# Output projection of a retention layer: ordinary products in phase one and block products in phase two, with the sums of phase two made under phase one

## The chip, the cores and the metric

The kernel runs on one core of a Trainium2 chip. The metric is the device time of one execution in microseconds (us), as the median of several runs. A lower time is better. The engines are named as in the profile: PE is TensorE (matmul), PEld its weight load, DVE is VectorE, ACT is ScalarE, POOL is GpSimd, and SP is SyncE, which here only issues DMAs.

## The reference, cut to what matters

The model has two layers in f32, one of retention and one of sliding-window attention (SWA), for a prompt of 1024 tokens and eight single decode tokens. Only the retention layer and the first thing that SWA does are touched by the change.

```python
def retention_layer(x, S0, g_norm, w_in, g_out, w_out):
    h = rmsnorm(x, g_norm)
    q, k, v, gate = split(h @ w_in)          # 4 heads, DK = 256, DV = 512
    o, S = retention_scan(q, k, v, S0)       # per chunk of 128 tokens and head:
    #   inner = (q k^T) * decay mask;  o = inner v + (q S) * decay;  S = g S + (k*decay)^T v
    o = rmsnorm(o, g_out) * silu(gate)       # width 4 * 512 = 2048
    return x + o @ w_out, S                  # w_out: 2048 x 1024
```

`o @ w_out` has 2048 inputs per token (four heads of 512) and 1024 outputs. The next layer starts with `rmsnorm(x) @ w_in_swa`.

## The kernel before, in words

**Numbers in two parts.** Every f32 operand of a product is split into a high part (type fp32r, made by a copy, mostly on ACT) and a low part (value minus high part, on POOL or DVE), and a product is three matmuls: high by high, high by low, low by high.

**Stages.** (1) The input projection of retention, to about 537 us of the span. (2) The retention itself, 32 steps: a step is one chunk of 128 tokens of one head; first heads 0 and 1 alternate over eight chunks (steps 0 to 15), then heads 2 and 3 (steps 16 to 31). (3) The output projection, eight sets. (4) SWA, from 886.6 us.

**A retention step.** On PE: the state's update (`S`, L998 to L1000), the output (`po`, L1002 to L1011), then three groups of products into PSUM tiles named `tr`: the transposes of the normalised output `on` of the step before (L104), the product of k and q of a coming chunk (L776) and its transposes. PSUM has two `tr` buffers. On the other engines, in the order that `others` (L1065) writes them: DVE multiplies the transposed output of step i-2 by the gate (`og`, L1062), makes the low part of the state (`Sl`, L1030), the mean square (`bss`, L1041; its power -0.5 is POOL's L119), the score tile `sT` (L793), the normalised output `on` (L1049) and the low part of k (`kl`, L788). POOL makes the low parts of v, of the scores and of q (L813, L803, L825). ACT makes the high parts. The order on every engine is the order of the program; nothing is reordered.

**The output projection.** The eight sets are two phases of four: phase one multiplies the gated output of heads 0 and 1 by its half of `w_out`, phase two that of heads 2 and 3. Set a of a phase makes the output columns 256 a to 256 a + 255, for all 1024 tokens in two halves t = 0, 1, with decode columns beside them. In a set the weight piece is a 2 x 2 block of quarters A11, A12, A21, A22, and the tokens' side is a 2 x 2 block B11, B12, B21, B22 (head by even or odd chunks).

- An *ordinary* set (`p_plain`, L1282) has eight slots of 24 matmuls, 192 in all; its weights are the four quarters.
- A *block* set (`p_prod`, L1263) uses the scheme with seven products instead of eight: 14 slots of 12 matmuls, 168 in all. It needs sums of weight quarters (S1 to S4, `p_sum`, on POOL) and sums of the tokens' side (T1 to T4), and its results are combined by more additions (`p_evac` and `p_pre`).

The operands of the tokens' side lie in seven cells for each t (in the tiles SA and SB), called B11, T2, T1, B21, T3, B22, T4. Before the change sets 4 and 5 (the first two of phase two) are ordinary, and the six others are block sets. So T1 to T4 of heads 0 and 1 have to exist when phase one begins: `x_items` (L1080) spreads that work over steps 6 to 31 in four portions. A portion reads the gated chunks that DMAs have put into the cells, makes four sums on DVE in the tile G0 (the rows `G<-G,SA` and the like of L1549), seven high parts on ACT and seven low parts on POOL (L1549). For phase two the gated chunks go to DRAM (`osc`) and come back; `split` and `t_sums` turn them into cells in sets 3 to 6.

**The plan.** `p_plan` (L1400) gives each slot a time by its count of matmuls, and each piece of work on ACT, DVE, POOL and SP a due time or a slot (`when`, `later`); the pieces are then written into the program between the slots in that order. Of set 0, `p_early` (L1502) prepares the weight pieces A11, S1, S2 and A12 under the last retention steps. `p_xr` (L1205) loads the residual input x of a set, four DMAs of 128 KB each for one t, and `p_xt` (L1210) transposes it on DVE into the tiles that the slot results are added to (names evc, evw, evx, evp in the profile, and rx, rp); before the change both halves go through one tile, `xr`. Sets of phase one leave partial results in DRAM, which sets of phase two load.

**Other work in set 7.** `kv_raw` and `kv_conv` (L1388, L1394) load and split the weights of SWA's keys and values (rows `kv<-ra,kv`, L1398). `a_load` and `a_split` (L1360, L1363) reload the normalised result of the layer and split it for SWA (DVE rows of L1369).

## Time and profile before

| what | value |
|---|---|
| time, median of 3 runs | 1325.73 us (1324.01 to 1327.58) |
| the profiled execution's own time | 1328.74 us |
| its span in the profile | 1326.9 us |
| mean granted PE clock | 0.986 |
| PE busy | 1275.2 us, 96% of the span |
| DVE, ACT, POOL busy | 790.1, 682.7, 797.9 us |
| retention, first state product to the first product of set 0 | 537.20 to 696.40 us |
| the eight sets of the output projection | 696.40 to 886.60 us |

Times in the trace count from the start of the span. A row of the timeline has a start, a duration, engine, line, operation and tiles, and in brackets the idle time of its engine just before it with what ended it (`<-`). A row of the windows has the stretch, its length, and for each engine busy time and count of instructions, then the granted PE clock as a share of full speed, the share of the DMA engines' time and GB/s.

### The profile page before, as it was taken

How to read it: one execution, taken by the hardware profiler on the slowest of the kernel's cores; microseconds unless marked ns; L12 is line 12 of the kernel's file. 1: busy time of each engine (PE TensorE's matmuls, PEld its weight loads, DVE VectorE, ACT ScalarE, POOL GpSimd, SP SyncE). 2: the span in 40 equal slices, each digit the busy share in tenths (PEclk: the TensorE clock that was granted, in tenths of full speed). 3: DMA queues.
4: the chain of work that ended last, by engine and by line, in shares of the span. 5: the costliest groups of instructions: out<-in, count | busy, mean ns of one | idle time of the engine just before them, and what ended most of it. 6: DMA issues, size and time to landing. Idle time of an engine off the chain costs nothing.

```text
span 1326.9 us, 26895 instructions
## 1 busy us (share of the span) xinstructions
PE 1275.2 (96%) x9767; PEld 1217.6 (92%) x9767; DVE 790.1 (60%) x1511; ACT 682.7 (51%) x1686; POOL 797.9 (60%) x935
## 2 busy tenths in 40 slices
PE   6999999999999999899898999989998999999998
PEld 6999999999999999777778989979998999998998
DVE  6944555666566763477674568584565666766321
ACT  5532445454455563578772244456576666666121
POOL 6654534555468998679895676556476766554000
PEclk9999999999999999899998999989998999999999
DMA  6314777667676863478756586543032111227232
GB/s 225 101 60 143 220 218 227 200 214 227 202 215 188 236 201 110 140 241 253 237 183 174 145 264 198 172 156 109 17 96 80 57 55 46 81 95 260 73 95 77
DMA packets 230322, 208.79 MB, mean 157 GB/s; under 512 B 32889, under 2 KB 206197, under 8 KB 230173
## 3 DMA queue, kind: packets, MB, share of 16 engines
q1 hardware_dynamic: 198192, 172.71, 43.2%
q10 hardware_dynamic: 31996, 34.36, 7.9%
q8 instruction: 77, 1.26, 0.4%
q14 instruction: 57, 0.46, 0.1%
HBM read 134.36 MB, written 69.50 MB: 154 GB/s over the span
## 4 chain that ended last, share of the span: by engine, by line
PE 78%; POOL 6%; DVE 5%; issue 4%; DMA 4%; ACT 2%; SPq 1%; POOLq 0%; ACTq 0%; DVEq 0%
PE b L334 8%; PE b L335 7%; PE b L336 7%; PE pj L1634 6%; PE pj L1635 5%; PE pj L1636 5%; PE b L327 4%; PE b L328 4%; PE b L329 4%; PE S L1293 3%; PE tr L104 3%; PE o L1997 2%; PE b L543 2%; PE S L336 1%; PE S L334 1%
## 5 line engine op out<-in xcount | busy, mean ns | idle before, releaser
L334 PE MATMUL b<-xh,woh 128*128 128x258 f32 x784 | 223.2, 285 | 0.0
L336 PE MATMUL b<-xh,wol 128*128 128x258 f32 x784 | 221.7, 283 | 0.0
L335 PE MATMUL b<-xl,woh 128*128 128x258 f32 x784 | 221.6, 283 | 0.0
L1634 PE MATMUL pj<-SA,wh 128*128 128x384 f32 (+1 forms) x512 | 175.0, 342 | 1.7 <-ACT SA L2017 1.3
L1635 PE MATMUL pj<-SA,wh 128*128 128x384 f32 (+1 forms) x512 | 164.8, 322 | 0.2 <-DVE SA L2018 0.2
L1636 PE MATMUL pj<-SA,wl 128*128 128x384 f32 (+1 forms) x512 | 164.7, 322 | 0.0
L334 PEld LDWEIGHTS b<-xh,woh 128*128 128x128 f32 x784 | 148.0, 189 | 4.1 <-issue 3.7
L335 PEld LDWEIGHTS b<-xl,woh 128*128 128x128 f32 x784 | 148.7, 190 | 0.0
L336 PEld LDWEIGHTS b<-xh,wol 128*128 128x128 f32 x784 | 148.0, 189 | 0.0
L225 POOL TENSOR_TENSOR wol<-raw,woh 128x512 fp32r<-128x512 f32 x52 | 68.0, 1316 | 119.8 <-ACT woh L220 108.6
L327 PE MATMUL b<-woh,xh 128*128 128x256 f32 x448 | 126.6, 283 | 0.0
L328 PE MATMUL b<-wol,xh 128*128 128x256 f32 x448 | 126.0, 281 | 0.0
L329 PE MATMUL b<-woh,xl 128*128 128x256 f32 x448 | 125.6, 280 | 0.0
L1634 PEld LDWEIGHTS pj<-SA,wh 128*128 128x128 f32 x512 | 97.1, 190 | 5.4 <-issue 2.6
L1635 PEld LDWEIGHTS pj<-SA,wh 128*128 128x128 f32 x512 | 97.3, 190 | 0.4 <-DVE SA L2018 0.4
L1636 PEld LDWEIGHTS pj<-SA,wl 128*128 128x128 f32 x512 | 96.9, 189 | 0.0
L1975 POOL TENSOR_TENSOR s<-s,sm 128x512 f32<-128x512 f32 x64 | 66.6, 1040 | 48.3 <-DVE sm L1974 44.1
L327 PEld LDWEIGHTS b<-woh,xh 128*128 128x128 f32 x448 | 84.3, 188 | 5.0 <-issue 2.9
L329 PEld LDWEIGHTS b<-woh,xl 128*128 128x128 f32 x448 | 84.3, 188 | 0.0
L328 PEld LDWEIGHTS b<-wol,xh 128*128 128x128 f32 x448 | 84.3, 188 | 0.0
L1967 ACT ACTIVATE s<-s,mx 128x257 f32<-128x257 f32 x128 | 64.2, 505 | 34.6 <-DVE mx L1965 33.8
L220 ACT ACTIVATE woh<-s 128x512 fp32r<-128x512 f32 x88 | 54.1, 624 | 53.3 <-POOL s L210 22.8
(543 smaller groups left out, 3823.6 us busy)
## 6 DMA issues: line engine op xcount, KB each, us to landing
raw<-in_w_in_ret_dram ACTq DMA_DIRECT2D x44, 512.0 KB
st<-in_state_ret_dram SPq DMA_DIRECT2D x64, 256.0 KB
out_dram<-st SPq DMA_DIRECT2D x64, 256.0 KB
vb<-vscr SPq DMA_DIRECT2D x64, 128.0 KB
evp<-qks SPq DMA_DIRECT2D x32, 256.0 KB
evx<-vsc SPq DMA_DIRECT2D x32, 256.0 KB
wr<-in_w_in_swa_dram SPq DMA_DIRECT2D x32, 256.0 KB
evc<-gsc SPq DMA_DIRECT2D x16, 256.0 KB
```

What stands on the lines that cost most here:

```text
L225: eng.tensor_tensor(lo, src_of(s, name, sub), hi.bitcast(F32), SUB)
L327: mm(dst, xh, wh, start=a and i == 0, stop=False, skip_group_check=True)
L328: mm(dst, xh, wl, start=False, stop=False, skip_group_check=True)
L329: mm(dst, xl, wh, start=False, stop=z, skip_group_check=True)
L334: mm(dst, wh, xh, start=a, stop=False, **sg)
L335: mm(dst, wh, xl, start=False, stop=False, **sg)
L336: mm(dst, wl, xh, start=False, stop=z, **sg)
L1634: mm(ps, hi[:, k, fs], xh[:, k, t0:t1], start=first and k == ks[0], stop=False)
L1635: mm(ps, hi[:, k, fs], xl[:, k, t0:t1], start=False, stop=False)
L1636: mm(ps, lo[:, k, fs], xh[:, k, t0:t1], start=False, stop=last and k == ks[-1])
L1967: nc.scalar.activation(st[:, j, :], st[:, j, :], AF.Exp, bias=mx[:, j:j + 1], accum_out=sm[:, j:j + 1])
L1975: nc.gpsimd.tensor_tensor(st[:, :, 0:256], st[:, :, 0:256], sm.unsqueeze(2).broadcast_to([128, 2, 256]), ALU.mult)
```

## The change

1. **The two phases change kind.** Sets 0 to 3 (phase one) are ordinary and sets 4 to 7 (phase two) are block sets.
2. **No sums under the retention.** `x_items` is gone. Each gated chunk of heads 0 and 1 stays in SBUF (`OG`) and is split right away into one cell by one ACT copy (`b_oh`) and one POOL subtraction (`b_ol`), two steps later than its products, 16 of each. The DMAs that put these chunks into the cells are gone.
3. **The sums of phase two are made under phase one.** The chunks of heads 2 and 3 are loaded from DRAM in sets 0 and 1 (2 MB into the cells T1 and T2, 2 MB into the two G tiles), and `t_sums`, now in six parts, makes T1, T2, T4 and a scratch copy of T3 in sets 1 and 2. B11 and B21 are split in set 3, T3 and B22 in set 4.
4. **Set 0 is prepared further.** `p_early` at steps 20 to 30 loads the raw weights, makes all four quarters (high on ACT, low on POOL) and loads x for t = 0 into a tile of its own (`acc`); x for t = 1 is loaded when the projection's tiles open. What belongs to the end of the retention comes after slot 0 instead of slot 1.
5. **Retention's buffers** are laid out one by one (`lay`), in a given order, which changes the addresses that they share with tiles of stage 1; the last two loads of v and gate of the start (`b_v(3)`, `b_g(3)`) are issued at step 0 instead of at the end of stage 1.
6. **SWA's key and value weights** are loaded and split in set 5 instead of set 7. Their raw tile is `xr`.
7. Smaller ones: x loads of sets 1 to 3 are issued 18 and 17 us ahead instead of 9 and 3 (`p_plan`'s time); `p_pre` is split into three; two of SWA's first small products are issued ahead of their loop.

The diff, cut to its core:

```diff
...
-    for fn, n in ((b_v, 2), (b_q, 3), (b_g, 2), (b_v, 3), (b_g, 3)):
+    for fn, n in ((b_v, 2), (b_q, 3), (b_g, 2)):
...
+    lay("Sh1", "Sl1", "sT0", "sTh0", "sTl0", "on0", "qh0", "ql0", "kh0", "kl0", "sT1", "ss0", "ss1", "vl0",
+        "on1", "vh1", "vl1", "kh1", "kl1", "pad", "Sh0", "Sl0", "vh0", "qh1", "ql1", "sTh1", "sTl1")
...
+        o_ = ogt[h % 2] if h >= 2 else OG[:, (2 * c + h) % 4]
         dve.tensor_tensor(o_, d.pop(("pt", c)).rearrange("p (i t) -> p i t", i=4), d["g", c], MUL)
-        nc.sync.dma_start(out=(osc[h - 2, par, t] if h >= 2 else raw_of(((B11, T1), (B21, B22))[h][par], t))[:, :, cs], in_=o_)
+        if h >= 2:
+            nc.sync.dma_start(out=osc[h - 2, c % 2, c // 4][:, :, 128 * (c // 2 % 2):128 * (c // 2 % 2) + 128], in_=o_)
+        d["og", c] = o_
+
+    def b_oh(h, c):
+        if h < 2:
+            act(at_cell(h, c)[0], heads[h]["og", c], AF.Copy)
+
+    def b_ol(h, c):
+        if h < 2:
+            hi, lo = at_cell(h, c)
+            pool.tensor_tensor(lo, heads[h]["og", c], hi.bitcast(F32), SUB)
...
-                      [(b_on, i - 1)] + conv[3:]):
+                      [(b_on, i - 1)] + conv[3:] + [(b_oh, i - 2), (b_ol, i - 2)]):
...
-        dec_sums(dT, 0)
...
-    def x_items(q, i0):
...
-        ta, tb, tc_ = [G0[:, 512 * j:512 * j + 512].rearrange("p (k f) -> p k f", k=4) for j in (q % 3, (q + 1) % 3, (q + 2) % 3)]
-        src = {B11: r[B11], B21: r[B21], B22: r[B22], T1: ta, T2: tb, T3: tc_, T4: ta}
...
-        for i, o_, x, y in ((0, ta, r[T1], r[B11]), (1, tb, r[B22], ta), (2, tc_, tb, r[B11]), (4, ta, r[B21], tb)):
-            put(i, dve.tensor_tensor, o_, x, y, SUB)
-        for i, x in enumerate((B22, T1, T2, B11, T3, B21, T4)):
-            put(i, act, XH[t][x][:, :, cs], src[x], AF.Copy)
-            put(i + 2, pool.tensor_tensor, XL[t][x][:, :, cs], src[x], XH[t][x].bitcast(F32)[:, :, cs], SUB)
...
-        s.n, s.P, s.a, s.kind, s.fw, s.plain = n, n // 4, n % 4, "p", 128, n in (4, 5)
+        s.n, s.P, s.a, s.kind, s.fw, s.plain = n, n // 4, n % 4, "p", 128, n < 4
...
+    def xr_tile(t):
+        return acc[:, 0:1024].rearrange("p (n f) -> p n f", n=16) if t == 0 else pq["xr"]
+
     def p_xr(s, t):
...
+            nc.sync.dma_start(out=xr_tile(t)[32 * b:32 * b + 32], in_=v[b])
 
     def p_xt(s, t):
...
+        for key in "cpxw":
             i, par = KEY[key]
             if t == 0:
-                if key in "cw":
-                    c_tile(s, key)
-                else:
-                    s.r[key] = pq["r" + key]
...
         if j == 2 and t:
-            later(n + 1 if s.n else n + 3, p_pre, s)
+            for m_, key in ((1, "w"), (3, "x"), (5, "p")):
+                later(n + m_, p_pre, s, key)
...
-        p_fins(s, key, t, n)
+        if t:
+            later(n + 2, p_store, s, key)
...
-            dve.tensor_tensor(b11, z, b11, SUB)
-        for n_, fn in enumerate((one, two, three)):
+
+        def four():
+            y, z, b11, b21 = b()
+            pool.tensor_tensor(y, b21, z, SUB)
+            dve.tensor_tensor(z, z, b11, SUB)
+
+        def five():
+            y, z, b11, b21 = b()
+            piece(T4, t, h, y)
+            nc.sync.dma_start(out=osc[0, 1, t][:, ks], in_=z)
+
+        def six():
+            piece(T4, t, h, b()[0], pool)
+        for n_, fn in enumerate((one, two, three, four, five, six)):
             later(k + n_, fn)
...
-                if s.n == 0 and name in ("A11", "S2", "S1", "A12"):
+                if s.n == 0:
...
-                    when(max(s.t0 - 22.0, 1.5) + 0.1 * j, p_raw, s, j)
+                    when(max(s.t0 - 22.0, 6.0) + 0.1 * j, p_raw, s, j)
             if s.P == 0:
-                a = s.t0 - 9.0 if s.n else 0.5
-                b = s.t0 - 3.0 if s.n else 5.0
-                when(a, p_xr, s, 0)
-                when(b, p_xt, s, 0)
-                when(b + 0.1, p_xr, s, 1)
-                when(b + 5.5, p_xt, s, 1)
+                if s.n:
+                    when(s.t0 - 18.0, p_xr, s, 0)
+                    when(s.t0 - 17.0, p_xr, s, 1)
+                when(s.t0 - 3.0 if s.n else 0.0, p_xt, s, 0)
+                when(s.t0 - 2.0 if s.n else 3.0, p_xt, s, 1)
...
-        n, m, m2 = psets[3].n0, psets[4].n0, psets[5].n0
-        q = psets[6].n0
...
+        later(n1, st_open)
+        later(n1 + 1, lambda: dec_sums(pq["dT"], 8))
         for t in range(2):
-            split(n + 3 + t, B11, t, 0)
-            split(n + 8 + t, B21, t, 1)
-            later(n + 9 + t, o_load, raw_of(T3, t)[:, :, 0:256], 0, 1, t)
-            later(n + 11 + t, o_load, raw_of(B22, t)[:, :, 0:256], 1, 1, t)
-            later(m, o_load, raw_of(T1, t)[:, :, 0:256], 0, 1, t)
-            later(m, o_load, raw_of(T2, t)[:, :, 0:256], 1, 1, t)
-            split((n + 13, m)[t], T3, t)
-            split(m + 1 + t, B22, t)
-            split(m2 + 3 + 2 * t, T4, t, 1)
-            split(q + 1 + 2 * t, T3, t, 0)
-        for k, x, plain in ((n + 4, B11, False), (n + 9, B21, False), (m, T3, True), (m + 2, B22, False), (m + 4, T1, False),
-                            (m + 5, T2, False), (m2 + 2, T4, False), (q + 2, T3, False)):
-            DC(k, x, plain)
-        for k in range(4):
-            t_sums((m + 3, m + 5, m + 7, m2 + 1)[k], k // 2, k % 2, k)
-        u = psets[7].n0
+            later(4 + t, o_load, raw_of(T1, t)[:, :, 0:256], 0, 1, t)
+            later(5 + t, o_load, raw_of(T2, t)[:, :, 0:256], 1, 1, t)
+            for h in range(2):
+                later(n1 + t, st_load, h, 0, t)
+                t_sums(n1 + 4 + 6 * t + 3 * h, t, h, 2 * t + h)
+            split(n3 + 4 + t, B11, t, 0)
+            split(n3 + 6 + t, B21, t, 1)
+            later(n3 + 6 + t, st_load, 0, 1, t)
+            later(m + t, st_load, 1, 1, t)
+            split(m + 1 + 2 * t, T3, t, 0)
+            split(m + 4 + 2 * t, B22, t, 1)
+        for k, x in ((n1 + 6, T1), (n1 + 7, T2), (n1 + 9, T4), (n3 + 4, B11), (n3 + 6, B21), (m + 1, T3), (m + 4, B22)):
+            DC(k, x)
         for k in range(6):
             later(u + 1 + k, a_load, k)
             later(u + 4 + k, a_split, k, 0)
             later(u + 5 + k, a_split, k, 1)
+        b = psets[5].t0
+        when(b + 1.0, kv_open)
         for j in range(2):
-            when(psets[6].t0 + 16.0, kv_raw, j)
-        when(psets[6].t0 + 15.0, kv_open)
+            when(b + 1.0 + 9.0 * j, kv_raw, j)
         for i in range(4):
-            when(psets[7].t0 + 1.4 * i - 1.0, kv_conv, i)
+            when(b + (6.0, 7.5, 15.0, 16.5)[i], kv_conv, i)
...
+            pq["e"] = [EO, gp.tile([128, 2048], F32R, tag="sga", name="E1")]
+        if n < 2:
+            p_raw(s, n)
+        elif n == 10:
+            p_xr(s, 0)
         else:
-            name = ("S2", "A12")[n - 4]
-            o_ = rp.tile([128, 2, DV], F32R, name="Sl", bufs=2).rearrange("p a (k f) -> p a k f", k=4)
-            p_hi(s, name, [o_[:, 0], o_[:, 1]])
-            p_lo(s, name)
+            i = (n - 2) // 2
+            name = ("A11", "A12", "A21", "A22")[i]
+            if n % 2 == 0:
+                p_hi(s, name, ops_in(pq["e"][i // 2][:, 1024 * (i % 2):1024 * (i % 2) + 1024]))
+            else:
+                p_lo(s, name, pool)
...
+    for n, x in enumerate((B11, B21, T3, B22)):
...
-            items.setdefault(9 + n + part, []).append((dec_cols, (dT, 0, x, part)))
+            items.setdefault(9 + n + part, []).append((dec_cols, (None, 0, x, part, True)))
...
-        if i in (20, 23, 26, 29, 31):
-            p_early((20, 23, 26, 29, 31).index(i))
+        if i == 0:
+            b_v(3)
+            b_g(3)
+        if i >= 20 and i < 31:
+            p_early(i - 20)
...
-        if n == 1:
+        if n == 0:
             others(NS)
             at_step(b_tr, NS - 1)
...
-            for i in sorted(items):
-                later(1 + i - NS, lambda its: [fn(*args) for fn, args in its], items[i])
-        for fn, args in (at.pop(n, ()) if n else ()):
+            p_xr(psets[0], 1)
+        for fn, args in at.pop(n, ()):
...
-        while n and ev and ev[0][0] < end:
+        while ev and ev[0][0] < end:
...
```

**Where the order of the work moves.** First, DVE in step 21 of the retention (head 3), as it was before (`G` is the tile of the sums, `og` the gated output, `tr` a PSUM tile, numbers behind a name belong to the tile).

```order
L1549 TENSOR_TENSOR G_7435<-G_7435,SA 128x512
L1062 TENSOR_TENSOR og<-tr,evw 128x512
L1030 SCALAR_TENSOR_TENSOR Sl<-S,Sh 128x512 x2
L1041 TENSOR_SCALAR bss<-bss,M_88 128x1
L793 TENSOR_TENSOR sT<-tr,M_7451 128x128
L1049 TENSOR_SCALAR on<-po,bss 128x512
L788 SCALAR_TENSOR_TENSOR kl<-tr,M_88,kh 128x256
```

The same stretch of DVE after the change (`ss` is what was `bss`):

```order
L1082 TENSOR_TENSOR og<-tr,evw 128x512
L1048 SCALAR_TENSOR_TENSOR Sl<-S,Sh 128x512 x2
L1058 TENSOR_SCALAR ss<-ss,M_88 128x1
L795 TENSOR_TENSOR sT<-tr,M_7447 128x128
L1066 TENSOR_SCALAR on<-po,ss 128x512
L790 SCALAR_TENSOR_TENSOR kl<-tr,M_88,kh 128x256
```

The row of L1549 ahead of `og` is gone; the other six kinds of rows stand in the same order.

Second, POOL in step 15 of the retention (the last of head 1), before (SA and SB hold cells):

```order
L803 TENSOR_TENSOR sTl<-sT,sTh 128x128
L825 TENSOR_TENSOR ql<-evp,qh 128x256
L1549 TENSOR_TENSOR SB<-G_7435,SB 128x4x128
L1549 TENSOR_TENSOR SB<-SB 128x4x128
L977 TENSOR_TENSOR SB<-dT,SB 128x2x4x2
L119 TENSOR_TENSOR bss<-bss,mhalf 128x1
L813 TENSOR_TENSOR vl<-evx,vh 128x512
```

POOL there after the change:

```order
L805 TENSOR_TENSOR sTl<-sT,sTh 128x128
L827 TENSOR_TENSOR ql<-evp,qh 128x256
L1094 TENSOR_TENSOR SA<-OG,SA 128x4x128
L119 TENSOR_TENSOR ss<-ss,mhalf 128x1
L815 TENSOR_TENSOR vl<-evx,vh 128x512
L805 TENSOR_TENSOR sTl<-sT,sTh 128x128
L1094 TENSOR_TENSOR SA<-OG,SA 128x4x128
```

Where there were two low parts of L1549 in a step, others having none, there is now one low part of L1094 in a step, straight from the gated chunk in `OG`.

Third, DVE where the retention ends and set 0 begins, before (S and b are PSUM tiles of the products, w weights' low parts, `xr` the loaded x):

```order
L1062 TENSOR_TENSOR og<-tr,evw 128x512
L1183 TENSOR_TENSOR evp<-S,evp 128x258
L1222 STREAM_TRANSPOSE evw<-xr 128x256
L1222 STREAM_TRANSPOSE evc<-xr 128x256
L1222 STREAM_TRANSPOSE rx<-xr 128x256
L1222 STREAM_TRANSPOSE rp<-xr 128x256
L1183 TENSOR_TENSOR evp<-S,evp 128x258
L1159 TENSOR_TENSOR w_9513<-s1a,w_9513 128x512
```

And after:

```order
L1082 TENSOR_TENSOR og<-tr,evw 128x512
L1233 STREAM_TRANSPOSE evc<-acc 128x256
L1233 STREAM_TRANSPOSE evp<-acc 128x256
L1233 STREAM_TRANSPOSE evx<-acc 128x256
L1233 STREAM_TRANSPOSE evw<-acc 128x256
L1307 TENSOR_TENSOR evc<-S,evc 128x258
L1233 STREAM_TRANSPOSE evc<-xr 128x256
L1233 STREAM_TRANSPOSE evp<-xr 128x256
L1233 STREAM_TRANSPOSE evx<-xr 128x256
L1233 STREAM_TRANSPOSE evw<-xr 128x256
L1307 TENSOR_TENSOR evc<-S,evc 128x258
```

The transposes of both halves of x, the first from `acc`, come ahead of all but one addition of a slot's result, and the low parts of weights (L1159) are gone from set 0 on DVE.

More of the change, by code (lines that the diff above doesn't have):

```diff
@@ L1015, in b_Sh @@
         if c < NCH - 1:
-            d["Sb"] = [rp.tile([128, 2, DV], F32R, name=nm, bufs=2) for nm in ("Sh", "Sl")]
+            d["Sb"] = [state(nm, h % 2) for nm in ("Sh", "Sl")]
             for f in range(2):
@@ L1034, in b_sq @@
         d = heads[h]
[L1035 to L1036 removed]
+        d["on", c], d["ss", c] = R["on"][h % 2], R["ss"][h % 2]
         act(d["on", c], d["po", c], AF.Square, accum_out=d["ss", c])
@@ L1524, in _trunk @@
     nc.sync.dma_start(out=M23, in_=a["c1"][:, 384:640])
-    for q, i0 in enumerate((6, 12, 18, 25)):
-        x_items(q, i0)
-    for n, x in enumerate((B11, T2, T1, B21, T3, B22, T4)):
+    for n, x in enumerate((B11, B21, T3, B22)):
         for part in range(2):
-            items.setdefault(9 + n + part, []).append((dec_cols, (dT, 0, x, part)))
+            items.setdefault(9 + n + part, []).append((dec_cols, (None, 0, x, part, True)))
     xdg = x_decode()
```

120 lines of the change are left out of this document (57 added, 63 removed).

## The prediction

> **What bounds the kernel now.** I read the windows by stage first, because the change touches only the stretch from 537 to 887 us. After the length, each row has the busy time of PE and its weight load, of DVE, ACT and POOL, then the granted PE clock, the DMA share and GB/s. The first two are the retention, then come sets 0, 3, 4, 6 and 7 of the output projection.
>
> ```profile
> 537.20:549.10 11.90, 7.14 (x35) 5.65 (x35) 4.21 (x9) 5.38 (x14) 6.35 (x12) 0.83 0.65 198
> 549.10:696.40 147.30, 137.97 (x727) 113.88 (x726) 109.73 (x222) 107.81 (x269) 127.85 (x158) 0.98 0.71 220
> 696.40:725.10 28.70, 23.63 (x175) 23.04 (x174) 13.26 (x32) 7.17 (x21) 16.34 (x13) 0.90 0.63 162
> 766.00:791.50 25.50, 22.24 (x170) 21.81 (x169) 14.65 (x24) 10.95 (x22) 16.71 (x15) 0.93 0.82 271
> 791.50:814.70 23.20, 23.20 (x194) 23.20 (x193) 17.48 (x23) 10.06 (x24) 16.42 (x14) 1.00 0.85 271
> 837.90:858.20 20.30, 20.30 (x170) 20.23 (x169) 12.95 (x22) 9.15 (x21) 14.25 (x11) 1.00 0.46 144
> 858.20:886.60 28.40, 24.04 (x170) 23.16 (x168) 22.88 (x28) 16.49 (x28) 17.66 (x11) 0.88 0.52 178
> ```
>
> PE is the bound: an undisturbed block set takes 20.30 us (set 6) and an undisturbed ordinary set 23.20 us (set 4), with PE busy throughout. Sets 0, 3 and 7 are block sets too, and are 8.4, 5.2 and 8.1 us over 20.30. Next I asked what PE waited for, in the retention and in the sets (total us, times, longest).
>
> ```profile
> PE tr L104 <- DVE on L1049: 11.4, 9, 3.0
> PE tr L776 <- issue: 2.3, 1, 2.3
> ```
>
> ```profile
> PE S L336 <- POOL w L1159: 7.8, 3, 3.2
> PE S L334 <- DVE evw L1188: 3.2, 2, 2.2
> ```
>
> The waits in the retention are for the normalised output, those in the sets for weights' low parts and for results that DVE has not taken away. They sum to 24.7 us, but sets 0, 3 and 7 alone are 21.7 us over. The rest is the clock:
>
> ```profile
> 617.51:620.91 3.40, 3.38 (x19) 2.63 (x19) 2.06 (x6) 2.85 (x8) 3.25 (x6) 1.00 0.94 299
> 647.50:650.90 3.40, 3.40 (x12) 2.72 (x11) 2.87 (x7) 2.48 (x7) 3.15 (x4) 0.50 0.54 169
> 719.20:726.00 6.80, 5.75 (x26) 5.75 (x27) 3.28 (x9) 1.64 (x6) 3.25 (x3) 0.50 0.51 139
> 787.50:790.90 3.40, 3.40 (x17) 3.40 (x17) 1.37 (x4) 2.01 (x4) 3.40 (x4) 0.50 1.03 345
> ```
>
> The last three rows are stretches at half clock just behind PE's stops of 3.02, 3.25 and 2.45 us (rows below). A stretch of 3.4 us at half clock does 1.7 us of work, so it costs 1.7 us. Behind the stop that ended at 617.51 the clock stayed at 1.00. So a stop longer than some two microseconds costs its length and 1.7 us more. In sets 0, 3 and 7 the mean clocks of 0.90, 0.93 and 0.88 say the same: 0.10, 0.07 and 0.12 of their lengths is 2.9, 1.8 and 3.4 us.
>
> **The change part by part.** *A, the steps of the retention.* The first state product of an undisturbed step comes 4.56 us after that of the step before; for the first chunk of heads 2 and 3 it is 3.49.
>
> ```profile
> 549.10 0.78 PE L998 MATMUL S<-vh,kh 128*128 128x512 f32 x1
> 554.98 0.47 PE L998 MATMUL S<-vh,kh 128*128 128x512 f32 x1
> 559.54 0.47 PE L998 MATMUL S<-vh,kh 128*128 128x512 f32 x1
> ...
> 618.56 0.48 PE L998 MATMUL S<-vh,kh 128*128 128x512 f32 x1
> 622.05 0.47 PE L998 MATMUL S<-vh,kh 128*128 128x512 f32 x1
> ```
>
> From 549.10 to 696.40 are 30 steps: 28 at 4.56 and 2 at 3.49 make 134.7, the window has 147.3, so 12.6 is over. Of this 1.3 is in the first of these steps (5.88), which belongs to B. The largest piece shows where the 11.3 comes from:
>
> ```profile
> 641.25 1.76 DVE L1549 TENSOR_TENSOR G<-G,SA 128x512 f32<-128x512 f32 x1 [2.38 <-POOL SB L1549]
> ```
>
> ```profile
> 646.56 0.63 PE L104 MATMUL tr<-ident,on 128*128 128x128 f32 x4 [3.02 <-DVE on L1049]
> ```
>
> DVE, in order, stands 2.38 us at a sum of `x_items` until POOL has made two low parts, then works 1.76 us on it; behind it are `og`, `Sl`, `bss`, `on`, and PE waits for `on`. These sums go away, so nothing on DVE waits for POOL's low parts. What is late next is POOL itself, which keeps one low part per step in steps 2 to 17, of the kind of the last row here (busy, mean ns):
>
> ```profile
> L813 POOL TENSOR_TENSOR vl<-evx,vh 128x512 fp32r<-128x512 f32 x30 | 38.7, 1289 | 5.8 <-ACT vh L808 5.8
> L825 POOL TENSOR_TENSOR ql<-evp,qh 128x256 fp32r<-128x256 f32 x28 | 22.0, 786 | 0.0
> L803 POOL TENSOR_TENSOR sTl<-sT,sTh 128x128 fp32r<-128x128 f32 x30 | 19.7, 656 | 0.0
> L119 POOL TENSOR_TENSOR bss<-bss,mhalf 128x1 f32<-128x1 f32 x31 | 17.1, 550 | 18.8 <-DVE bss L1041 18.8
> L1549 POOL TENSOR_TENSOR SA<-G,SA 128x512 fp32r<-128x512 f32 x8 | 9.6, 1202 | 0.0
> ```
>
> 1.29 + 0.79 + 0.66 + 0.55 + 1.20 = 4.49 us against 4.56. It fits, barely; the first-chunk steps (3.70 without `ql`, against 3.49) and some small decode columns don't. I leave 2.3 of the 11.3: A = −9.0. Bounds: all of it (−11.3), or −1 if POOL overruns (below). The four weight pieces of set 0 put four such low parts into steps 23 to 29, which have no other, so they are covered by the same 4.56.
>
> *B, the start of the retention.* ACT stands at `qh` until a DMA has read the tile `raw`, whose addresses `qh` takes over; kh, then kl and PE are late behind it. PE stops twice, 2.50 us and the 2.3 us of the waits above.
>
> ```profile
> 544.76 0.81 PE L104 MATMUL tr<-ident,on 128*128 128x128 f32 x4 [2.50 <-DVE on L1049]
> ```
>
> ```profile
> 545.91 0.42 ACT L819 ACTIVATE qh<-evp 128x256 fp32r<-128x256 f32 x1 [5.66 <-DMA gsc<-raw]
> ```
>
> In the new layout `raw` lies under the states Sh1, Sl1, which are needed a step later than `qh`. The second stop should go, the first stays: −2.3, and −0.4 for the part of its slow stretch in the next step. B = −2.7; bounds 0, if the states' copy stands at the same DMA and the rest of ACT behind it, and −6.1 (2.5 + 2.3 + 1.3).
>
> *C, set 0.* Three waits follow one another: x is asked for only when the set runs, comes 6 us later, and the weights' low parts stand behind the transposes on DVE, or behind POOL's sums.
>
> ```profile
> 701.47 2.24 SPq L1208 DMA_DIRECT2D xr<-in_x_prompt_dram  x4
> ```
>
> ```profile
> 707.43 0.45 DVE L1222 STREAM_TRANSPOSE evw<-xr 128x256 f32<-128x256 f32 x1 [5.45 <-DMA xr<-in_x_prompt_dram]
> ```
>
> ```profile
> 720.25 0.58 PE L336 MATMUL S<-SB,w 128*128 128x258 f32 x1 [3.25 <-POOL w L1159]
> ```
>
> All four weights are now ready before the set, x for t = 0 is loaded under step 30, and x for t = 1 about 6 us after slot 0, while results may wait for some slots of 2.9 us (23.20 / 8) each. So 8.4 over becomes about 1.0: C = −7.4 (−8.4 to −4).
>
> *D, one block set less, twice.* Ordinary sets go from two to four: 2 × (23.20 − 20.30) = +5.8. This is sure, as PE has no other way to do 192 instead of 168 matmuls.
>
> *E, set 3.* Its longest stop is for a weight's low part, which POOL makes late behind the splits of B11 and B21.
>
> ```profile
> 787.28 0.43 PE L336 MATMUL S<-SB,w 128*128 128x258 f32 x1 [2.45 <-POOL w L1159]
> ```
>
> The set becomes ordinary and needs no weight sums, but set 4, now the first block set, needs T3 and B22 reloaded and split as it begins. I leave 1.5: E = −3.7 (0 to −5.2).
>
> *F, set 7.* POOL works off the SWA weights and comes late with its own:
>
> ```profile
> 867.58 1.74 POOL L1159 TENSOR_TENSOR w<-rb,w 128x512 fp32r<-128x512 f32 x1
> ```
>
> ```profile
> L1398 POOL TENSOR_TENSOR kv<-ra,kv 128x512 fp32r<-128x512 f32 x4 | 5.2, 1304 | 4.8 <-ACT kv L1397 4.8
> ```
>
> ```profile
> L1369 DVE SCALAR_TENSOR_TENSOR SA<-SA,gcol 128x1024 fp32r<-128x1024 f32 x6 | 10.4, 1741 | 0.0
> ```
>
> The 5.2 us and POOL's wait of 4.8 go; DVE's 10.4 us of splits stay, and with them results taken away late (the 3.2 us of waits at L334). Half of 8.1 goes: F = −4.1 (−1 to −8.1). In set 5 POOL has 14.25 + 5.2 = 19.45 of 20.30 by the row of set 6: +0.7 (0 to +3). Set 1 was within 0.3 of 20.30, −0.3.
>
> **Sum:** −9.0 − 2.7 − 7.4 + 5.8 − 3.7 − 4.1 + 0.7 − 0.3 = −20.7. The profiled execution's own 1328.74 becomes 1308.0. It lies 3.0 above the median of the runs, so the median is forecast at 1325.73 − 20.7 = **1305**.
>
> Of these terms some 9 us are clock, not waiting: 1.7 in A, 0.4 in B, 2.9 in C, 1.8 in E and 1.7 (one stretch of two) in F. [...]
>
> **The rivals.** (1) *POOL overruns in the retention.* Its operations lengthen where other engines are busier: 1.74 instead of 1.29 us for the low part in set 7, above. At 11% longer the 4.49 become 4.98, and steps 2 to 17 each lose some 0.4 to 0.5: 16 × 0.5 = 8. Against it: from 549 to 696 POOL was already busy for 127.85 of 147.30, and the row of L1549 is from there. Time 1305 + 8 = 1313. (2) *The half clocks stay though the stops go*, because something else than the stops makes them: 9 of the 20.7 are lost, 1314. Against it: each begins where a stop ends. (3) *Set 4 stands at T3 and B22*, as set 3 did at B11: E is 0, and with set 5's POOL at its bound (+2.3) the time is 1311. (4) *Slower: x comes late in each later ordinary set.* SP issues its DMAs in order, and in sets 0 and 1 the loads of T1, T2 and G (4 MB) stand ahead of x; those for G must also wait until set 0's weights, at the same addresses, are used up. DVE would wait at the transposes with everything behind them, as in set 0 before, at 8.4 a set: 3 × 8.4 = 25, 1330. It decides once x lands about 6 us later than I reckon (some 41 us after the start of set 0, for transposes that are due at 47, both my estimates). Against it: sets 3 and 4 moved 271 GB/s, and set 4 lost nothing at a DMA share of 0.85. (5) *Nothing comes of it:* the loads and sums that move under phase one stop PE there for as long as they did elsewhere, 1326.
>
> **How the numbers follow.** Forecast 0.50, rivals (1) 0.15, (2) 0.08, (3) 0.11, (4) 0.10, (5) 0.06. The forecast's own range is 1296 to 1316: downwards half of what the bounds leave (A 2.3, B 3.4, C 1.0, E 1.5, F 4.0, together 12.2; more is possible but all at once unlikely, so 9), upwards 11 for two of the terms at their worse ends. Rivals 1 to 3 lie inside or near it. I give 1296 to 1322, which leaves out (4), (5) and a small rest below. A measurement of this kernel can tell about 0.3%, 4 us, from no change. Faster: 0.50 + 0.15 + 0.08 + 0.11 = 0.84; no change 0.06; slower 0.10.
>
> **What would show it.** A: 30 steps in about 137 us, and PE's waits for `on` (now `ss` ahead of it) down from 11.4 to some 2. If POOL has no idle time and steps 2 to 17 take 5 us, it is rival 1. B: no stop ahead of the product of k and q near 546. C: set 0 in about 24 us, no wait of PE for a weight in it. D: four windows of 23.2 and, undisturbed, 20.3. E and F: stops of PE in the first third of set 4, and in set 7 only for results (`ev` tiles). Rival 2: clock 0.50 with no stop ahead. Rival 4: DVE's transposes waiting for `xr` or `acc` in sets 1 to 3, with PE idle behind. The prediction is wrong if the stretch from the retention's start to the end of set 7, 349.4 us now, comes out above 345 or below 319.

## The result and the profile after

The changed kernel takes 1314.45 us as the median of four runs (1313.32 to 1317.08), the kernel before 1326.65 us in the runs beside them. The ratio is 0.9912 with a 95% interval of 0.9887 to 0.9937: 12.2 us less, clear of noise, where 20.7 were forecast. The profiled execution took 1315.55 us with a span of 1313.6, which is 13.3 less than the span before.

The windows of the changed kernel's profile, cut at its own stages: the first two steps of the retention, its other thirty (to the first product of set 0 at 684.46), phase one, phase two, and the 47.8 us behind the last product of set 7. Columns as in the prediction.

```profile
539.09:548.22 9.13, 6.12 (x34) 5.04 (x35) 3.15 (x7) 5.48 (x14) 6.09 (x12) 1.00 0.85 254
548.22:684.46 136.24, 133.97 (x730) 112.67 (x728) 96.92 (x205) 101.62 (x255) 109.14 (x143) 1.00 0.68 210
684.46:777.81 93.35, 93.35 (x776) 93.35 (x774) 50.13 (x94) 24.93 (x60) 36.67 (x35) 1.00 0.78 224
777.81:864.20 86.39, 81.92 (x674) 81.03 (x672) 57.38 (x90) 41.75 (x85) 60.47 (x43) 1.00 0.60 177
864.20:912.00 47.80, 37.68 (x266) 35.54 (x266) 18.54 (x65) 19.57 (x69) 21.12 (x30) 0.93 0.28 81
```

And the same length behind set 7 in the kernel before:

```profile
886.60:934.40 47.80, 45.15 (x341) 43.44 (x342) 22.78 (x77) 26.42 (x82) 29.00 (x40) 1.00 0.39 116
```

The thirty steps fell from 147.30 to 136.24 us. Phase one has no idle PE at all: 93.35 us for four ordinary sets and the last transposes of the retention. Phase two takes 86.39, some 5 over four times 20.30. So from the start of the retention to the end of set 7 it is 325.1 us instead of 349.4, a gain of 24.3, more than the 20.7 of the forecast. The last row shows where the rest went: in the first 47.8 us of SWA PE now does 266 matmuls where it did 341. From the end of set 7 to the end of the span it is 449.4 us instead of 440.3: 9.1 are given back. Another 1.9 lie ahead of the change: the first state product of step 0 comes at 539.09 instead of 537.20. −24.3 + 9.1 + 1.9 = −13.3, the difference of the spans.

PE's waits in the retention of the changed kernel, which were 11.4 us in nine waits for `on`:

```profile
PE tr L104 <- DVE on L1066: 3.5, 2, 3.0
PE tr L778 <- issue: 1.5, 1, 1.5
```

PE's waits behind set 7 in the kernel before:

```profile
PE pj L1737 <- DVE evx L1188: 1.1, 1, 1.1
PE tr L104 <- DVE kkl L1764: 1.1, 1, 1.1
PE pj L1634 <- DVE kd L1719: 0.4, 1, 0.4
```

And in the changed kernel:

```profile
PE pj L1757 <- DVE kd L1739: 3.3, 1, 3.3
PE pj L1757 <- DVE evx L1203: 2.3, 1, 2.3
PE sc L1757 <- ACT wh L1626: 2.3, 1, 2.3
PE pj L1654 <- ACT wh L1626: 0.8, 1, 0.8
```

The two long ones that are new stand at products of SWA's keys and values (L1757) for results of chunks that came before (the second is put down to ACT, but the product starts behind DVE's kd of chunk 1, the last row here):

```profile
881.66 0.36 PE L1757 MATMUL pj<-kv,SA 128*128 128x256 f32 x1 [3.29 <-DVE kd L1739]
...
888.76 0.36 PE L1757 MATMUL sc<-kv,SA 128*128 128x256 f32 x1 [2.28 <-ACT wh L1626]
```

```profile
888.01 0.61 DVE L1739 SCALAR_TENSOR_TENSOR kd<-sc,krk,kgb 128x128 f32<-128x128 f32 x2 [1.21 <-POOL krk L1737]
```

### The profile page after: what moved, and what is told of

It reads as the page before. It is cut to its first block, busy times and chain, and to the rows that moved or that the text cites. A ratio compares the mean times of both kernels' runs of the same rounds, so it can differ in the third digit from the quotient of the medians.

```text
span 1313.6 us, 26814 instructions
## 1 busy us (share of the span) xinstructions
PE 1271.3 (97%) x9815; PEld 1217.2 (93%) x9815; DVE 764.5 (58%) x1475; ACT 668.7 (51%) x1656; POOL 754.3 (57%) x903
## 4 chain that ended last, share of the span: by engine, by line
PE 84%; POOL 5%; DVE 3%; ACT 3%; issue 2%; DMA 2%; SPq 0%; ACTq 0%; POOLq 0%; DVEq 0%
PE S L1301 7%; PE b L334 7%; PE b L336 7%; PE b L335 7%; PE pj L1654 6%; PE pj L1655 6%; PE pj L1656 6%; PE b L327 4%; PE tr L104 4%; PE b L328 4%; PE b L329 4%; PE o L2017 2%; PE b L543 2%; PE sc L1980 1%; PE S L336 1%
```

## The experiments

### Where the gain was given back: the order of SWA's first products

Theory: the smallest edit of the change, two products issued ahead, with all later ones two chunks early. Even chunks use the PSUM tiles `pj`, odd ones `sc`, and there are two buffers of each. So the first half of chunk 4 (`pj`) must wait until the results of chunk 0 have been taken away, and PE, in order, makes everything else wait with it. Rival: DVE and ACT at the end of set 7 set the start of SWA, whatever the order. Three kernels: the order undone in the changed kernel, the early halves kept for chunks 0 to 3 alone, and the new order alone in the kernel before.

```diff
 swa_order_undone (from the changed kernel)
-    kv_mm(0, 0)
-    kv_mm(1, 0)
     for n in range(9):
-        if n < 7:
-            kv_mm(n + 2, 0)
+        kv_mm(n, 0)

 swa_lead_four (from the changed kernel)
     for n in range(9):
-        if n < 7:
+        if n < 2:
             kv_mm(n + 2, 0)
+        elif n >= 4:
+            kv_mm(n, 0)

 before_swa_ahead (from the kernel before)
+    kv_mm(0, 0)
+    kv_mm(1, 0)
     for n in range(9):
-        kv_mm(n, 0)
+        if n < 7:
+            kv_mm(n + 2, 0)
```

> The changed kernel, with the first small products of SWA (the keys and values of a chunk) issued again one chunk at a time inside their loop, as before the change. Theory: the new order makes PE stand, in order, at the first half of chunk 4, whose PSUM buffer is still held by chunk 0, and this gives back about 10 us of what retention and projection gained; so the time falls from 1314.5 to 1303 to 1307, PE's waits for kd of 3.3 and 2.3 us near 880 and 889 are gone, and the end of set 7 stays where it is (864 us of the span). Rival: DVE and ACT at the end of set 7 set the start of SWA in any order; then 1312 to 1316.

> The changed kernel, with the first halves of chunks 0 to 3 issued ahead as in the change, but those of chunks 4 to 8 in their own turn, so that no product stands ahead of others while its PSUM buffer is held. Theory: the harm is in the lead of chunks 4 to 8 alone, and the early halves fill idle time of PE while DVE finishes set 7: 1300 to 1305, at or below the kernel with the order undone. Rival (the early start as such harms, because the row that makes the norms of x comes later on PE): 1307 to 1315.

> The kernel before, with the changed order of SWA's first products and nothing else. Theory: the order costs the same 8 to 10 us here, 1334 to 1337. Rival (it costs only behind a set 7 that ends early): 1324 to 1328.

| kernel | median us | ratio to before, 95% interval |
|---|---|---|
| swa_order_undone | 1307.73 | 0.9849 (0.9809 to 0.9889) |
| swa_lead_four | 1308.48 | 0.9862 (0.9826 to 0.9899) |
| before_swa_ahead | 1334.45 | 1.0052 (1.0034 to 1.0069) |

The kernel before was 1327.27 there. Undoing the order gives 6.7 us back against the changed kernel's 1314.45, and the order alone costs the kernel before 7.2. The long waits are the same in both places. PE's waits behind set 7 of before_swa_ahead:

```profile
PE pj L1737 <- DVE kd L1719: 3.3, 1, 3.3
PE pj L1737 <- DVE evx L1188: 2.3, 1, 2.3
PE sc L1737 <- ACT wh L1606: 2.3, 1, 2.3
PE pj L1634 <- ACT wh L1606: 0.8, 1, 0.8
```

With the order undone the 3.3 for kd and the 2.3 at `sc` are gone. PE's waits in the same stretch of swa_order_undone:

```profile
PE pj L1757 <- DVE evx L1203: 2.3, 1, 2.3
PE tr L104 <- DVE kkl L1784: 1.2, 1, 1.2
PE pj L1654 <- DVE kd L1739: 0.4, 1, 0.4
PE tr L104 <- DVE kd L1739: 0.3, 1, 0.3
```

PE does 326 matmuls in these 47.8 us. The windows of swa_order_undone, then of before_swa_ahead:

```profile
864.20:912.00 47.80, 43.68 (x326) 41.59 (x326) 21.57 (x75) 25.61 (x81) 27.86 (x39) 1.00 0.38 115
```

```profile
885.10:932.90 47.80, 37.86 (x266) 35.72 (x267) 18.37 (x65) 19.76 (x70) 21.11 (x30) 0.93 0.29 81
```

So the theory holds: the order costs about 7 us, somewhat less than the 10 expected, and it costs them with the old set 7 too. The rival falls. From the end of set 7 to the end of the span swa_order_undone takes 441.9 us, against 449.4 in the changed kernel and 440.3 before. So the order accounts for 7.5 of the 9.1 us that were given back. The wait of 2.3 for `evx` stays, and it is 1.2 longer than before; no run takes that apart. swa_lead_four shows that the harm is in the lead of chunks 4 to 8. Its 1300 to 1305 were missed: that the early halves of chunks 1 to 3 fill idle time and win something beyond was not seen (1308.5 against 1307.7, overlapping). This lies in the rival's range, but level with swa_order_undone, so the early start as such does no harm that can be told. PE waits 1.9 us at one of them for `evp` instead of later. swa_order_undone beats both kernels.

It was run again beside two other kernels, for which it is the base:

> The same kernel as the run swa_order_undone, for a comparison on one chip with the two others: 1306 to 1309, with the first state product of step 0 anywhere between 537.0 and 539.1 us, if the 1.9 us by which stage 1 ended later in the changed kernel's profile are only a difference between executions.

1308.9 us (ratio 0.9848, 0.9815 to 0.988). The first state product of step 0 came at 537.28 in its profile, and at 538.76 in the first run of the same kernel. In the eleven profiles after the change it lay between 537.0 and 539.3, so the 1.9 us ahead of the retention are a difference between executions and not of the change.

### The retention: how near POOL is to its limit

My step A left POOL as what is late next: 4.49 of 4.56 us per step. The first rival was that it overruns. The low parts were made twice, then moved to DVE.

```diff
 low_parts_twice (from the changed kernel)
             pool.tensor_tensor(lo, heads[h]["og", c], hi.bitcast(F32), SUB)
+            pool.tensor_tensor(lo, heads[h]["og", c], hi.bitcast(F32), SUB)

 low_parts_on_dve (from the changed kernel)
-            pool.tensor_tensor(lo, heads[h]["og", c], hi.bitcast(F32), SUB)
+            dve.tensor_tensor(lo, heads[h]["og", c], hi.bitcast(F32), SUB)
```

> The changed kernel, with each low part of a gated chunk made twice on POOL (16 subtractions more, steps 2 to 17). By the rows of POOL it is busy 4.1 to 4.3 of 4.57 us in such a step; with 1.2 us more it would need 5.3 to 5.5, so these steps become 0.7 to 1.0 longer and the time rises by 11 to 16 us. Rival: POOL's order leaves slack that the busy time does not show, or PE waits less than POOL is late: under 5 us more.

> The changed kernel, with these low parts made on DVE instead of POOL. DVE is busy 3.35 of 4.57 us in a step and gets one operation of about 0.7; POOL falls to some 3.0. If POOL near its limit cost nothing in the changed kernel (my step A), the retention's steps stay at 4.57 and the time within 2 us. Rival 1 of the prediction (POOL's load costs time): steps 2 to 17 get shorter, by 2 us or more in all; and if DVE's order matters more than its busy time, they get longer, by 0.3 to 0.7 each.

low_parts_twice took 1330.43 us in one run, 16 more. The first state products of steps 12 and 13 in the timelines, in low_parts_twice and then in the changed kernel:

```profile
602.72 0.48 PE L1016 MATMUL S<-vh,kh 128*128 128x512 f32 x1
...
608.20 0.48 PE L1016 MATMUL S<-vh,kh 128*128 128x512 f32 x1
```

```profile
595.77 0.48 PE L1016 MATMUL S<-vh,kh 128*128 128x512 f32 x1
...
600.36 0.47 PE L1016 MATMUL S<-vh,kh 128*128 128x512 f32 x1
```

5.48 us against 4.59. From step 0 to step 31 the retention is 13.4 us longer. Behind the stop of 3.0 at its start PE waits 10.5 us in 15 waits for `on`, against 0.5 in one in the changed kernel. So one low part of 1.20 us more is paid by 0.89: POOL had about 0.3 us left per step, and not 0.07. The rows of POOL agree. Two of its operations take less time than before the change, the low part of the scores (656 ns before) and that of q (786). Groups of POOL in the changed kernel's retention:

```profile
L815 POOL TENSOR_TENSOR vl<-evx,vh 128x512 fp32r<-128x512 f32 x30 | 38.8, 1295 | 4.2 <-ACT vh L810 4.1
L827 POOL TENSOR_TENSOR ql<-evp,qh 128x256 fp32r<-128x256 f32 x28 | 20.5, 732 | 0.0
L119 POOL TENSOR_TENSOR ss<-ss,mhalf 128x1 f32<-128x1 f32 x32 | 17.6, 550 | 26.8 <-DVE ss L1058 26.7
L805 POOL TENSOR_TENSOR sTl<-sT,sTh 128x128 fp32r<-128x128 f32 x30 | 13.8, 460 | 0.0
L1094 POOL TENSOR_TENSOR SA<-OG,SA 128x512 fp32r<-128x512 f32 x8 | 9.6, 1196 | 0.0
```

Their means sum to 4.23 us. low_parts_on_dve took 1316.16 in one run, and steps 8 to 15 stayed at 4.57 to 4.60 (steps 6 and 7 became 0.2 longer each). POOL's load therefore costs the changed kernel nothing in these steps, though it would from about 0.3 us more on.

### The start of the retention

My step B: the second stop came from the addresses of `qh` over the tile `raw`. One kernel puts `qh` and `ql` back there, another puts the loads of chunk 3 back ahead of the DMAs that empty `raw`.

```diff
 qh_over_raw (from the changed kernel)
-    lay("Sh1", "Sl1", "sT0", "sTh0", "sTl0", "on0", "qh0", "ql0", "kh0", "kl0", "sT1", "ss0", "ss1", "vl0",
-        "on1", "vh1", "vl1", "kh1", "kl1", "pad", "Sh0", "Sl0", "vh0", "qh1", "ql1", "sTh1", "sTl1")
+    lay("qh0", "qh1", "ql0", "ql1", "Sh1", "Sl1", "sT0", "sTh0", "sTl0", "on0", "kh0", "kl0", "sT1", "ss0", "ss1", "vl0",
+        "on1", "vh1", "vl1", "kh1", "kl1", "pad", "Sh0", "Sl0", "vh0", "sTh1", "sTl1")

 start_loads_undone (from swa_order_undone)
-    for fn, n in ((b_v, 2), (b_q, 3), (b_g, 2)):
+    for fn, n in ((b_v, 2), (b_q, 3), (b_g, 2), (b_v, 3), (b_g, 3)):
...
-        if i == 0:
-            b_v(3)
-            b_g(3)
```

> The changed kernel, with only qh and ql laid first, so that they lie over the tile raw again as before the change. My step B: ACT stands at qh until the DMA has read raw, and the second stop of PE (2.3 us ahead of the product of k and q, near 546) comes back: the first state product of step 2 is 2 to 3 us later after that of step 0 (9.1 us now, 11.9 before). Rival: the loads moved to step 0 removed that stop, not the addresses: 9.1 stays.

> The kernel with SWA's order undone, with the loads of v and gate of chunk 3 issued again at the end of stage 1, ahead of the DMAs that empty raw. If the loads' place alone had removed PE's second stop at the start of the retention, and not the new addresses, then raw is emptied some 3 us later again, but now only the high state Sh1 lies over it, which ACT needs late: no second stop, and step 5's wait for v (1.2 to 1.5 us near 567, in every run with the loads moved) is gone: 1306 to 1307 against 1307.7. Rival: ACT stands at Sh1 and everything behind it is late, a stop of 1 to 2.5 us near 552: 1308 to 1310.

In qh_over_raw ACT stands at `qh` for 0.45 us, where it stood 5.66 before, and the second stop does not come back. (It took 1320.04 us in one run. Step 2 begins 10.1 us after step 0, not 9.1, but with half clock behind the first stop (0.50 in 546.50 to 550.00), which is another matter, at the end of this document.) SP and ACT in its timeline:

```profile
541.13 1.91 SPq L396 DMA_DIRECT2D gsc<-raw  x3
```

```profile
544.61 0.42 ACT L821 ACTIVATE qh<-evp 128x256 fp32r<-128x256 f32 x1 [0.45 <-DMA gsc<-raw]
```

From the first state product (539.04 in this execution) `raw` is asked to be emptied 2.1 us later and is empty by 5.6. Before (537.20) it was 3.0 and 8.7. So the loads' place brings the emptying 3 us forward, the rival's cause. But with the loads back and the new addresses the stop did not come either. ACT in start_loads_undone:

```profile
547.58 1.08 ACT L1036 ACTIVATE Sh<-S 128x512 fp32r<-128x512 f32 x2 [0.78 <-DMA gsc<-raw]
```

`raw` is late again (8.3 us from 539.33), and it costs ACT 0.78 at the state, and PE nothing. So either part of the change removes the stop by itself; my step named one of the two. What I expected of step 5 was wrong: its stop (1.2 to 1.5 us, with v's loads late) stands at 1.29 in start_loads_undone too, so the loads' place does not make it. ACT stands there for a load of v (rows in the part on the prediction); why that load is late is open. start_loads_undone took 1308.22 us (0.9853, 0.9833 to 0.9874), not to be told from its base.

### Set 0: x or the weights

```diff
 x_of_set0_late (from the changed kernel)
         elif n == 10:
-            p_xr(s, 0)
+            pass
...
+            p_xr(psets[0], 0)
             p_xr(psets[0], 1)
```

> The changed kernel, with x for t = 0 of set 0 asked for when the projection's tiles open (as x for t = 1 is), not under step 30. Theory: what cleared set 0 is mostly that its weights are ready; results may wait four slots of 2.9 us for x, so PE stops in set 0 for 1 to 3 us in all and the time rises by 1 to 3 us. Rival (x was the cause): PE stops for 5 to 8 us in set 0, as before the change.

One run took 1318.52 us, 4.1 above the median of the changed kernel. DVE's first transpose then waits 6.23 us for x in set 0, and PE does not stop in set 0 at all: the results wait in PSUM, as reckoned. PE stops in set 1. DVE, ACT and PE in this kernel's timeline:

```profile
696.30 0.45 DVE L1233 STREAM_TRANSPOSE evc<-acc 128x256 f32<-128x256 f32 x1 [6.23 <-DMA acc<-in_x_prompt_dram]
```

```profile
709.24 0.67 ACT L1169 ACTIVATE w<-rb 128x512 fp32r<-128x512 f32 x1 [21.02 <-DMA rb<-in_w_out_ret_dram]
```

```profile
712.40 1.24 PE L1301 MATMUL S<-SA,w 128*128 128x258 f32 x8 [1.69 <-ACT w L1169]
```

The four more loads of x stand on SP's queue ahead of set 1's raw weights, and these come late: they are asked for at 705.73 instead of 700.30, with 1.3 us of this for the set's later start in this execution. So x under step 30 is not what cleared set 0. What is left is the weights that are ready before the set; that is by elimination, as no run makes them late. x under step 30 clears the queue for set 1. The stops there are 1.9 us. Half clock behind the first stop of the retention and behind the stop in set 7 comes in some executions without this edit (0.50 in start_loads_undone and in low_parts_on_dve, at the end of this document), so one run does not say what else of the 4.1 is the edit's.

### Set 7: the SWA weights and DVE's splits

Two kernels on top of swa_order_undone: the key and value weights back in set 7, and (with the start's loads undone) one of DVE's six splits given to ACT and POOL.

```diff
 kv_split_in_set7 (from swa_order_undone; the raw weights go through ra again)
...
-        b = psets[5].t0
-        when(b + 1.0, kv_open)
         for j in range(2):
-            when(b + 1.0 + 9.0 * j, kv_raw, j)
+            when(psets[6].t0 + 16.0, kv_raw, j)
+        when(psets[6].t0 + 15.0, kv_open)
         for i in range(4):
-            when(b + (6.0, 7.5, 15.0, 16.5)[i], kv_conv, i)
+            when(psets[7].t0 + 1.4 * i - 1.0, kv_conv, i)

 pool_takes_a_split (from start_loads_undone)
             act(A_hi[:, k, 0:NP], lo_.bitcast(F32), AF.Copy, scale=gk)
+            if k == 3:
+                act(pq["xr"].rearrange("p n f -> p (n f)"), lo_.bitcast(F32), AF.Copy, scale=gk)
+        elif k == 3:
+            pool.tensor_tensor(lo_, pq["xr"].rearrange("p n f -> p (n f)"), A_hif[:, k, 0:NP], SUB)
...
-            later(u + 5 + k, a_split, k, 1)
+            later(u + (11 if k == 3 else 5 + k), a_split, k, 1)
```

> The kernel with SWA's order undone (1307.7 us), with the key and value weights of SWA loaded and split in set 7 again instead of set 5. My step F: POOL comes late with set 7's weights again, PE stops there some 2 us for a low part and 2 us more at results, and set 5's stop near 818 (1.2 us) is gone: 1310 to 1313. Rival: the start of SWA hangs on DVE's own splits at the end of set 7, so POOL's 5.2 us there cost nothing: 1306 to 1309.

> As the run start_loads_undone, and one of DVE's six splits of the layer's result at the end of set 7 (k = 3, 2.0 us there) is made by ACT (the scaled value, into the free tile xr) and POOL (the subtraction), which is idle after 859. If DVE's splits are what is left of set 7's 8 us, as step F says, PE's stop of 2.25 us for results near 860 falls below 0.5 and the time by 1.5 to 2.5 us to 1304 to 1305.5. Rival: the stop goes, but DVE's additions after the last product set the start of SWA as before: 1306 to 1307.

kv_split_in_set7 took 1309.74 us (0.9864, 0.9834 to 0.9894) against 1307.73 and 1308.9 of its base: slower by 1 to 2 us, within the intervals, and between what was expected and the rival. Its stops in set 7 are clear. PE in its timeline:

```profile
850.77 0.38 PE L336 MATMUL S<-SA,w 128*128 128x258 f32 x1 [0.88 <-POOL w L1174]
...
863.75 0.55 PE L334 MATMUL S<-SB,w 128*128 128x258 f32 x1 [4.31 <-DVE evw L1203]
```

The stop for results is 4.31 instead of 2.25, and the stop of set 5 (0.7 to 1.2) is gone. So step F's trade shows in the stops, about 3 us in set 7 against 1 in set 5, while the time shows no difference that can be told.

pool_takes_a_split took 1307.42 us (0.9845, 0.9827 to 0.9863): no gain that can be told. PE's stops for results in set 7 did not fall but rose, from 2.4 us in two in its base start_loads_undone to 4.7 in two. The first (2.31) is that of the base (2.19). The reason for the second (2.35 instead of 0.25) stands in POOL's and DVE's timelines:

```profile
859.74 3.33 POOL L1395 TENSOR_TENSOR SA<-xr,SA 128x1024 fp32r<-128x1024 f32 x1
```

```profile
859.50 1.36 DVE L1397 SCALAR_TENSOR_TENSOR SA<-SA,gcol 128x1024 fp32r<-128x1024 f32 x1
860.78 2.57 DVE L1261 SCALAR_TENSOR_TENSOR SA<-evw,gcol,SA 128x256 fp32r<-128x256 f32 x1
863.27 0.41 DVE L1203 TENSOR_TENSOR evw<-S,evw 128x258 f32<-128x258 f32 x1
```

DVE's operation of L1261 takes 0.47 us where POOL is idle (at 854.93 and 864.80) and 2.57 here, until 0.3 us after POOL's subtraction has ended. The work taken off DVE came back as 2.1 us more for this one operation beside POOL.

## Why the prediction was right and wrong

The direction and the range (1296 to 1322) held. The gain was 12.2 us instead of 20.7.

- **The step that failed is the list of steps.** The sum ended at set 7 and had no term for item 7 of the change, two of SWA's products issued ahead. By the order undone it cost 6.7 us, and 7.2 alone in the kernel before. Without it the gain is 19.5 us (1327.27 to 1307.73) where 20.7 were forecast, so the terms that were listed come close as a sum. The question that step B asked of `qh` and `raw` (who holds the buffer, and what stands behind the waiting instruction) would have priced it.
- **A (−9.0): right.** The 29 steps behind step 2 went from 141.4 to 131.6 us, −9.8. The waits for `on` fell from 11.4 to 3.5, and 3.0 of those belong to B. The 2.3 that I left for POOL was not POOL, which had about 0.3 us to spare per step. What stayed is a stop of 1.5 at step 5: ACT stands for a load of v, and kh, kl and PE are late behind it:

```profile
566.02 0.63 ACT L810 ACTIVATE vh<-evx 128x512 fp32r<-128x512 f32 x1 [2.84 <-DMA evx<-vsc]
...
567.63 0.68 PE L778 MATMUL tr<-evp 128*128 128x128 f32 x4 [1.51 <-issue]
```

- **B (−2.7): −4.0, the right stop with half its cause.** The two steps and the next went from 11.90 + 5.88 to 9.13 + 4.60. Addresses and loads each remove the stop alone. The 1.3 of step 2 is the clock's, and luck: with a clock of 1.00 behind the first stop the step takes 4.60 in the changed kernel, with 0.50 there (545.13 to 551.95) it took 5.88 before, and two of the later kernels have 0.50 behind that stop again (qh_over_raw in 546.50 to 550.00, start_loads_undone in 547.66 to 551.06).
- **C, D and E together with sets 1 and 2, and F:** phase one and phase two were forecast to lose 9.0 us in all (C, D, E, F, +0.7 and −0.3), and went from 190.2 to 179.7, −10.5. C was mis-sized by its 1.0 that I left: PE does not wait in phase one. D is 2 × (23.34 − 20.30) = 6.1 instead of 5.8, with 93.35 / 4 = 23.34, the retention's last transposes included. E left 1.3 instead of 1.5, at a weight's low part that POOL makes at the end of set 4 and not at a reload (POOL has worked without a pause since 789.06, on a split of set 4's operands too, so these may have a part in it; no run tells):

```profile
796.83 0.39 PE L336 MATMUL S<-SB,w 128*128 128x258 f32 x1 [1.31 <-POOL w L1174]
```

- **F:** of 4.0 left, a stop of 2.25 and one of 0.17 stayed, for results, as forecast. kv in set 5 cost a stop of 0.73, forecast 0.7.
- **The clock** gave more than the 9 us that I counted in this profile: by the clock column the windows of before lost some 13 us to it, and after the change every window up to the end of set 7 stands at 1.00. But the stops of 3.01 and 2.25 us are still there, and in other kernels with the same code there they are followed by half clock (below). So some of the 24.3 is luck of this execution; the experiments that repeat that stretch took 325.4 to 328.8 us for it (swa_order_undone, its repeat, start_loads_undone and pool_takes_a_split).
- **The rivals:** (1) is refuted at the load that the kernel has, and shown to begin about 0.3 us further. (2) is not what happened in this execution, where no half clock is left up to the end of set 7. (3) and (4) are refuted by the stops listed above: none at a reload, none in phase one at a DMA share of 0.78. (5) fell with the gain.

## What to carry to other kernels

Price every edit, the smallest ones too: work that is issued earlier on an in-order engine must own its buffer when its turn comes, and here two products moved forward took back over a third of what the other edits had won. A stage gains by what leaves the in-order engine in front of the bound, not by how much busy time falls; measure the margin of the engine that comes next by giving it its work twice. Before moving work from DVE to POOL, look in the timeline how long DVE's operations take beside POOL's there: here one of 0.47 us took 2.57.

## What the runs showed of the hardware

**The same stop, another clock.** The prediction took half clock behind any stop of more than some two microseconds. The stop of 2.25 us in set 7 is the same in the changed kernel and in low_parts_on_dve. The row of PE in low_parts_on_dve, then the windows behind the stop in each, in this order:

```profile
860.25 0.55 PE L334 MATMUL S<-SB,w 128*128 128x258 f32 x1 [2.25 <-DVE evw L1203]
```

```profile
860.25:863.65 3.40, 3.40 (x16) 3.40 (x17) 3.40 (x6) 2.56 (x5) 0.00 (x0) 0.50 0.26 77
```

```profile
860.75:864.15 3.40, 3.23 (x24) 2.97 (x24) 3.40 (x6) 2.58 (x5) 0.00 (x0) 1.00 0.26 77
```

Once 0.50, once 1.00. The stop of 3.0 us at the start of the retention behaves alike: full clock in the changed kernel (1.00 in 547.13 to 550.53), half in start_loads_undone (0.50 in 547.66 to 551.06). PE's wait of 3.29 for kd had full clock behind it (1.00 in 881.66 to 885.06), while that of 2.29 for evx, 15 us earlier, had half (0.50 in 866.26 to 869.66). So the length of a stop does not decide by itself.

What goes with the clock in the traces of the kernel before and of the changed kernel is where the stop lies. In the kernel before half clock begins at 545.13, 647.53, 719.21, 787.47, 869.39 and 883.05, for 3.41 or 6.83 us each time, and all these lie a whole number of times 3.413 us behind the first (30, 51, 71, 95 and 99 times, to within 0.03). Cut from there into intervals of 3.413 us, its trace shows a clock of 0.50 or 1.00 in each of 372 intervals from 20 to 1290 us, and nothing between. So does the trace of the changed kernel, with a grid of its own (half clock from 866.25, and from 890.14 and 992.54, 7 and 37 times behind it). On that grid two intervals share the stop of 2.25 us. In low_parts_on_dve the clock was 1.00 up to 860.10 and 0.50 from 860.25, and the 3.41 us ahead of 860.22 hold the stop but for its last 0.03. The window ahead of the fall in low_parts_on_dve, then the two in the changed kernel:

```profile
856.81:860.22 3.41, 1.19 (x11) 0.98 (x9) 3.41 (x5) 1.25 (x3) 2.08 (x1) 1.00 0.11 31
```

```profile
856.01:859.42 3.41, 2.49 (x21) 2.28 (x19) 3.41 (x3) 2.17 (x4) 3.38 (x2) 1.00 0.15 41
859.42:862.84 3.42, 1.92 (x14) 1.74 (x15) 3.42 (x7) 1.83 (x3) 0.00 (x0) 1.00 0.14 38
```

Between 530 and 960 us the kernel before and the changed kernel have eight falls, and PE was busy for 0.48 to 1.47 us of the interval ahead of each, as for 1.19 in low_parts_on_dve. Where it was busy for 1.66 or more of an interval at full clock, the clock stayed, in both intervals of the wait of 3.29 too (1.89 and 1.66). That is no rule: near the end of the span both kernels fell behind an interval with PE busy throughout (1268.75 to 1272.16 before the change, 1255.37 to 1258.78 after it). No run here was made to test it.

**DVE beside POOL.** The 0.47 us operation that took 2.57 beside POOL's 3.33 us was the surprise of the last experiment. POOL starts at 859.74, DVE's operation, which reads evw and SA, at 860.78, and DVE ends 0.3 us behind POOL. So does the same operation at 857.42, with 1.22 us beside a POOL operation of 1.29 that starts at 857.06. Why it takes longer there, no run shows. POOL's low part of the scores went from 656 to 460 ns when DVE's sums left the retention; whether that has the same cause, no run here took apart.
